# An order planner that lets VectorE and GpSimd exclude each other, four operands moved to PSUM, and one more projection pair ahead of a pointwise product

## The chip, the core and the metric

The kernel runs on one core of a Trainium2 chip. The metric is device time in microseconds (us) of one execution; lower is better. The core has five engines with queues of their own: PE (TensorE, matmuls and transposes), DVE (VectorE), ACT (ScalarE), POOL (GpSimd) and SP (SyncE, which here only issues DMAs). An engine works through its own queue strictly in the order in which the program was written, so one late operand holds back everything behind it.

## What is computed

One layer over 2048 tokens of width 1024, with 16 learned meta tokens put in front:

```
u = rms_norm(h, pre_g)
glu_a, glu_b, conv_gate, q, k, v, sb_gate = split(u @ w_in)      # 7 x 512 columns
c = glu_a * sigmoid(glu_b)
c = silu(layer_norm(causal_depthwise_conv(c, 31 taps)))
c = (c @ w_pw2 + b_pw2) * silu(conv_gate)
s = stick_breaking_attention(q, k, v) * silu(sb_gate)            # 8 heads x 64
out = h + rms_norm(concat[c, s] @ w_out, post_g)
```

All of it is float32. Each product is made from three matmuls of high and low parts (hi x hi, hi x lo, lo x hi), so every operand is split: ACT copies it to a rounded type (`uh`, `hi`, `ah`), and DVE or POOL subtracts that from the original (`ul`, `lo`, `al`).

## The kernel before

**Tiles and stages.** The tokens are worked in four chunks of 512 columns (`TC`), channels on the 128 partitions. For each chunk: `in_proj` forms the glu pairs (`pairs`: the sigmoid half `G_B`, then the linear half `G_A`, for four groups `j` of 128 channels), then k, v and q; `attention` is the main stream of the chunk; beside it run, as filling work, `sb_gate`, the output projection of the chunk before, `conv_norm`, and `tail`, which holds `conv_gate`, a number of glu pairs of the next chunk (`BEFORE[c + 1]`, line 75), `conv_out` (the product with `w_pw2`, "pw2" for short) and the rest of the next `in_proj`. One projection group is 8 x 3 matmuls of 512 columns.

**The turn.** The normalised input of a chunk lies in two tiles `uh` and `ul`, of which there is one each. While the last `conv_gate` group of a chunk uses part k of them, `renew` asks for part k of the next chunk: `part_in` lets ACT write `uh` and DVE write `ul` by a SCALAR_TENSOR_TENSOR whose two wide operands, `t` and `uh`, lie in SBUF. The next pair needs these parts at once.

**The rates.** The row of rms rates of a chunk is made on PE by transposing a column broadcast along the free axis (`spread` for chunk 0, `spread_later` for the others), copied by ACT from PSUM into the SBUF tile `row`, and multiplied by DVE into the eight 128x512 parts of the input: `times` for chunk 0 (tiles `pr`, eight), `scale` for the others (tiles `tok`, eight a chunk). Chunk 0 starts before its rates are known: its first three pairs run on unscaled parts, and `once_more` forms the parts again from the scaled ones.

**Who does what.** DVE does the convolution as 31 taps for most groups (`conv`, run in the PSUM bank `cv`), the scans of the attention (`pr`) and most low parts; POOL does the low parts of the weights (`w<-wr,w`, but for the seven slabs named in `FIRST`, which DVE does), the taps of some groups (`conv_apart`), and a few sums. `swish` in `conv_norm` lets ACT write a sigmoid into an SBUF tile `ev`, and DVE combines it with the normalised value. In `meta_keys` the contribution of the meta tokens comes from PE in a PSUM tile `pj`; DVE adds it to the attention output `sr` and multiplies by the gate `gt`, both in SBUF.

**PSUM.** Eight banks of 128x512: two named `mm` (projections), four named `T`, taken in turn (attention scores, transposes, and what else needs a bank for a moment), one `av` (attention output of a head) and one `cv` (running convolution).

**What sets the order.** The program is written out by a planner that keeps an account of every engine's time. `Engine.issue` charges each instruction with a cost (`pe_cost`, `dve_cost`, `act_cost`, `pool_cost`), begins it when its engine is free in the account and its operands are ready in the account, and notes when its result will be there. `merge` takes the next piece of the main, the filling or the extra stream, whichever is ready by the account, keeping the two first to a pace given in `SHARES`; `step` runs pending small operations when they are ready and adds convolution taps while the account has DVE less than 1.5 us (`LAGS`) ahead of PE. So a wrong cost does not change a result: it changes the order in which the engines' queues are written, and where PE then finds an operand late. Nearly all instructions are written by line 211 (`issue`), which is why the profile's rows are told apart by their tiles.

Of the kernel before, what the change touches and what calls it, by code (L numbers as in the profile page):

```python
# [19 lines left out]
P = 128  # L20
# [3 lines left out]
NM = 16  # L24
# [47 lines left out]

BEFORE = 0, 1, 0, 0

SHARES = (
    [(29.8, 169.2)], [(73.1, 214.4)], [(116.0, 214.4)], [(125.1, 97.4), (160.4, 126.3)],
# [8 lines left out]
class Clock:  # L87
# [3 lines left out]
    def __init__(self):  # L91
        self.ready, self.used, self.free, self.rings, self.bufs = {}, {}, {}, {}, {}
        self.dma = 0.0
        self.soon = []

        self.here = ()
# [71 lines left out]
class Engine:  # L168
# [7 lines left out]
    def __getattr__(self, name):  # L176
        call = getattr(self.engine, name)

        def issue(out, *args, **kw):
            c = self.clock  # L180
            outs = [out] + [kw[k] for k in ("accum_out",) if k in kw]
            ins = [a for a in (*args, *kw.values()) if hasattr(a, "ap")]

            for a in (*ins, *outs):
                for e in c.writers(a, c.here):
                    self.run(e)
            for a in outs:
                for e in c.readers(a, c.here):
                    self.run(e)
            near = [a for a in ins if a.space != DRAM]  # L190
            when = max([c.at(a) for a in near] + [c.free.get(out.name, 0.0)]) + self.wait
            if self.gap:
                self.gap(when)
            n = max(int(np.prod(a.shape[1:])) for a in (out, *args) if hasattr(a, "shape"))
            busy, late = self.cost(name, n, kw)
            start = max(self.now, when)
            self.now = start + busy
            self.work += busy
            done = self.now + late
            if name == "dma_start":  # L200
                size = 4 * int(np.prod(out.shape))
                c.dma = max(c.dma, start + 1.6) + size / 370e3
                done = c.dma + 0.7
                if start > 30.0:
                    done += 2.5 if out.name.startswith("wr") else 1.0
            for a in outs:
                c.ready.setdefault(a.name, {})[extent(a)] = done
            for a in (*outs, *near):
                late = 3.0 if a.name.startswith("wr") and start > 30.0 else 0.0
                c.used[a.name] = max(c.used.get(a.name, 0.0), done + late)  # L210
            return call(out, *args, **kw)  # L211

        return issue


def pe_cost(name, n, kw):
    return max(4.5e-3 + n * 4.41e-4, 0.108 if n >= 64 else 0.06), 0.19


def dve_cost(name, n, kw):  # L220
# [39 lines left out]
def trunk(ctx: ExitStack, tc: tile.TileContext, x, xturn, xlater, meta, cpack, post_g, wpack, out):  # L260
# [272 lines left out]
                there.add(key)  # L533
            order.append((key, n, kept, save))
    todo_w = deque(order)
    FIRST = [len(order) - i - 1 for i in (0, 2, 3, 4, 5, 6, 7)]
    whole = [key for key, n, kept, save in order if not kept]
    at = {key: i for i, key in enumerate(slab_keys())}
    todo_raw = deque(whole)
# [100 lines left out]
    def load_first_in():  # L640

        uh, ul = u_now
        load_raw(1)
        sp.dma_start(cp, cpack)
        mt = T("pr", [P, KD, NM], PR)
        sp.dma_start(mt, xturn[:, :, :NM])
        keep["turned", 0] = 0
        ts = []  # L650
        for k in range(KD):
            ts.append(T("pr", [P, TC], PR))
            sp.dma_start(ts[k], xturn[:, k, NM:])
            when(lambda k=k: part_in(0, k, ts[k], uh, ul), [ts[k], cp])
            if k == 0:
                load_raw(2)

        def meta_in():
            hi, lo = uh[:, :, 0:NM], ul[:, :, 0:NM]
            act.activation(hi, mt, AF.Copy)  # L660
            dve.tensor_tensor(lo, mt, hi.bitcast(F32), op=ALU.subtract)

        def meta_times():
            dve.tensor_tensor(
                mt, mt, preg.unsqueeze(2).to_broadcast([P, KD, NM]), op=ALU.mult
            )
            meta_in()
            keep["meta"] = True

        when(meta_times, [mt, cp])  # L670
        load_raw()
        measured = []

        def fetch(i):
            t = tok()
            for b in range(2):
                tb = 2 * i + b
                sp.dma_start(t[:, b], x[tb * P : (tb + 1) * P, :])
                when(lambda b=b, tb=tb: measure(t[:, b], tb), [t[:, b]], tag="ev")

        def fetch_meta():
            m = T("q2", [P, D], 2)[:NM]
            sp.dma_start(m, meta)
            when(lambda: measure(m, NTB), [m], tag="ev")

        fetch(0)
        fetch_meta()
        when(lambda: fetch(1), [], date=7.5)

        def measure(t, tb):  # L690
            n = t.shape[0]
            junk = T("ev", [P, D], EV, BF16)
            act.activation(
                junk[:n], t, AF.Square, scale=D ** -0.5, accum_out=squares[:n, tb : tb + 1]
            )
            measured.append(tb)
            if len(measured) == NTB + 1:
                when(rates, [squares], [rate0])

        def rates():  # L700
            pool.tensor_scalar(squares, squares, 1e-6, None, op0=ALU.add)
            pool.tensor_tensor(
                rate0, squares, nhalf.to_broadcast([P, NTB + 1]), op=ALU.pow
            )
            when(spread, [rate0], [row])

        def spread():
            pt = PT("cv", [P, TC])
            for tb in range(NTB):
                pe.transpose(  # L710
                    pt[:, tb * P : (tb + 1) * P], rate0[:, tb : tb + 1].to_broadcast([P, P]),
                    ident,
                )
            pm = PT("av", [P, TC])[:, :NM]
            pe.transpose(
                pm, rate0[:NM, NTB : NTB + 1].to_broadcast([NM, P]), ident[:NM, :NM]
            )
            act.activation(row[:, NM:], pt, AF.Copy)
            act.activation(row[:, :NM], pm, AF.Copy)
            keep["row"] = True  # L720
            for go in waiting:
                go()
            for k in range(KD):
                when(
                    lambda k=k: times(k), [ts[k], row], [ts[k]], dve, pe.now + 3.0 + 1.5 * k
                )
            dve.tensor_tensor(
                mt, mt, row[:, :NM].unsqueeze(1).to_broadcast([P, KD, NM]), op=ALU.mult
            )

        scaled = []

        def times(k):
            dve.tensor_tensor(ts[k], ts[k], row[:, NM:], op=ALU.mult)
            scaled.append(k)

        def once_more(k):

            if k == 0:
                keep["turned", 0] = 0  # L740
                when(meta_in, [mt], date=pe.now)
            when(lambda: part_in(0, k, ts[k], uh, ul), [ts[k]], date=pe.now)

        keep["scaled"] = lambda: "row" in keep and len(scaled) == KD
        keep["once more"] = once_more
# [33 lines left out]

    def to_spread(c):  # L780
        if ("half", c) in keep and ("rates", c) in keep:
            when(lambda: spread_later(c), [later], [row], tag="T")

    def times_rate(c, k):
        t = xs[c, k]
        when(lambda: scale(c, k, t), [t, row], [t])

    def scale(c, k, t):
        dve.tensor_tensor(t, t, row[:, NM:], op=ALU.mult)
        keep["scaled", c, k] = True  # L790
        renewed(c)

    def spread_later(c):
        pt = PT("T", [P, TC])
        for tb in range(NTB):
            n = (c - 1) * NTB + tb
            pe.transpose(
                pt[:, tb * P : (tb + 1) * P], later[:, n : n + 1].to_broadcast([P, P]), ident
            )
        act.activation(row[:, NM:], pt, AF.Copy)  # L800
        keep["row", c] = True
        for k in range(KD):
            if (c, k) in xs:
                times_rate(c, k)
# [307 lines left out]
    def conv_norm(c, accs):  # L1112
# [56 lines left out]
                )  # L1169
        yield need(given=lambda: len(done) == 2 * NJ)  # L1170
        def swish(j):
            b, y, sg = lnb[:, j : j + 1], accs[j], ev()[:, :TC]
            act.activation(sg, y, AF.Sigmoid, bias=b)
            when(
                lambda: dve.scalar_tensor_tensor(y, y, b, sg, op0=ALU.add, op1=ALU.mult),
                [y, sg], [y],
            )

        for j in range(NJ):
            when(  # L1180
                lambda j=j: swish(j), [accs[j]], [accs[j]], date=pe.now + 1.5 * j, tag="ev"
            )
        keep["normed", c] = True

# [293 lines left out]
    def meta_keys(c, h0, h1, mixs):  # L1478
# [66 lines left out]
        for j in js:  # L1545
# [6 lines left out]
            pe.matmul(pj, vm[:, 0, j, :], al, start=False, stop=False)  # L1552
            pe.matmul(pj, vm[:, 1, j, :], ah, start=False, stop=True)
            hold.difference_update((sr.name, gt.name))
            dve.tensor_tensor(sr, pj, sr, op=ALU.add)
            dve.tensor_tensor(sr, sr, gt, op=ALU.mult)
            hi = T("mixs", [P, TC], 8, F32R)
            lo = T("mixs", [P, TC], 8, F32R)
            split(sr, hi, lo)
# [409 lines left out]
```

## Time and profile before

| | |
|---|---|
| median of 3 runs | 1333.38 us (1331.79 to 1334.39) |
| the profiled execution | 1335.07 us |
| its span, first to last instruction | 1333.2 us |
| instructions | 21888 |
| PE, PE weight load, DVE, ACT, POOL busy | 97%, 84%, 77%, 55%, 50% of the span |
| mean granted TensorE clock | 0.993 of full |
| DMA | 300.76 MB, mean 226 GB/s |

The span leaves out 1.9 us around the first and last instruction. "Busy" of PE counts matmuls whose ends are modelled, so a wait shorter than a matmul's modelled tail does not show as idle time. A row of instruction groups reads: line, engine, operation, tiles out <- in, shape, count | busy us in all, mean ns of one | idle time of the engine just before them and what ended it. A row of the timeline reads: start, duration, engine, operation, tiles, count, and in brackets the idle time before it with what ended it. A row of waits reads: us in total, times, longest us. In rows of windows every engine has its busy time with its count of instructions, then come the granted clock, the share of time the DMA engines moved data, and GB/s.

### The profile page before, as it was taken

The page shows a single profiled execution, that of the slowest core. Times are in us where ns is not written, and L with a number is a line of the kernel's source. Part 1 is how long each engine was busy: PE and PEld are TensorE (multiplying, and loading weights), DVE is VectorE, ACT ScalarE, POOL GpSimd, SP SyncE. Part 2 cuts the span into 40 slices and gives each one's busy share as a digit, 9 for nine tenths or more (in the row PEclk, how much of TensorE's full clock was granted, in tenths as well). Part 3 has the DMA queues.
Part 4 walks back from the last instruction along what each step waited for, and adds up shares of the span by engine and source line. Part 5 has one row for each costly group of instructions (what it writes and reads, how often), then busy time and mean ns, then how long its engine had stood idle before and what let it go on. Part 6 is the DMA issues. An engine that isn't in the chain of part 4 may idle for free.

```text
span 1333.2 us, 21888 instructions
## 1 busy us (share of the span) xinstructions
PE 1299.6 (97%) x7498; PEld 1115.9 (84%) x7498; DVE 1025.9 (77%) x1438; ACT 735.0 (55%) x1470; POOL 667.3 (50%) x780
## 2 busy tenths in 40 slices
PE   8899998999999999999999999999999999999995
PEld 8898886888789987888889988888877899988895
DVE  4999987998993488984586478885549889798864
ACT  6444454444455443567745444578776566655542
POOL 3545466777667631688831242399787121231400
PEclk9999998999999999999999999999999999999998
DMA  6676885899978995676755697666666556686644
GB/s 227 197 248 214 252 266 197 305 312 323 319 239 261 289 344 180 192 240 221 248 190 176 174 337 222 180 184 217 196 197 210 156 149 181 196 277 199 207 147 155
DMA packets 167470, 300.76 MB, mean 226 GB/s; under 512 B 17840, under 2 KB 72304, under 8 KB 167360
## 3 DMA queue, kind: packets, MB, share of 16 engines
q1 hardware_dynamic: 154208, 253.49, 61.4%
q0 software_dynamic: 13152, 45.88, 9.0%
q8 instruction: 59, 0.97, 0.3%
q14 instruction: 51, 0.42, 0.1%
HBM read 221.85 MB, written 77.46 MB: 225 GB/s over the span
## 4 chain that ended last, share of the span: by engine, by line
PE 84%; DVE 8%; DMA 3%; ACT 2%; issue 1%; POOL 1%; DVEq 0%; SPq 0%; POOLq 0%; ACTq 0%
PE mm L211 54%; PE T L211 20%; PE av L211 9%; DVE ul L211 2%; DVE tok L211 2%; DVE pr L211 1%; DVE cv L211 1%; DMA ev<-x 1%; DMA w<-wscr 1%; ACT ev L211 1%; DMA out<-tok 0%; DMA tok<-xlater 0%; PE cv L211 0%; DMA wr<-wscr 0%; DVE al L211 0%
## 5 line engine op out<-in xcount | busy, mean ns | idle before, releaser
L211 PE MATMUL mm<-uh,w 128*128 128x512 f32 (+1 forms) x1936 | 622.3, 378 | 4.5 <-DVE ehl L211 2.8
L211 PEld LDWEIGHTS mm<-uh,w 128*128 128x128 f32 x1936 | 354.7, 190 | 65.5 <-DVE ehl L211 2.8
L211 PE MATMUL mm<-ul,w 128*128 128x512 f32 (+1 forms) x968 | 362.7, 375 | 5.3 <-DVE ul L211 5.3
L211 DVE TENSOR_TENSOR al<-T,ah 128x512 fp32r<-128x512 f32 (+3 forms) x323 | 194.5, 602 | 142.3 <-ACT ah L211 140.9
L211 DVE TENSOR_TENSOR_SCAN pr<-T,pr,zcol 128x512 f32<-128x512 f32 x192 | 245.1, 1277 | 45.9 <-ACT T L211 43.5
L211 ACT ACTIVATE ah<-T 128x512 fp32r<-128x512 f32 (+3 forms) x323 | 171.7, 532 | 170.6 <-PE T L211 169.5
L211 DVE SCALAR_TENSOR_TENSOR cv<-ct,cp,cv 128x512 f32<-128x512 f32 x319 | 239.2, 750 | 7.0
L211 ACT ACTIVATE T<-T 128x512 f32<-128x512 f32 (+2 forms) x320 | 167.5, 525 | 95.2 <-PE T L211 91.5
L211 POOL TENSOR_TENSOR w<-wr,w 128x512 fp32r<-128x512 f32 x133 | 174.9, 1319 | 89.3 <-ACT w L211 88.1
L211 POOL TENSOR_TENSOR acc<-acc,pd 128x512 f32<-128x512 f32 x150 | 195.3, 1302 | 42.7 <-ACT pd L211 36.3
L211 PEld LDWEIGHTS mm<-ul,w 128*128 128x128 f32 x968 | 184.2, 190 | 34.5 <-DVE ul L211 8.6
L211 PE MATMUL T<-kk,q 128*128 128x512 f32 (+2 forms) x640 | 194.8, 387 | 1.5 <-DVE pr L211 1.4
L211 PE MATMUL T<-ident,pr 128*128 128x128 f32 x1088 | 171.2, 272 | 0.3 <-DVE al L211 0.2
L211 PEld LDWEIGHTS T<-ident,pr 128*128 128x128 f32 x1088 | 134.1, 140 | 31.3 <-DVE al L211 1.0
L211 DVE TENSOR_TENSOR_SCAN pr<-T,tri 128x128 f32<-128x128 f32 (+3 forms) x128 | 103.8, 814 | 19.5 <-ACT T L211 18.4
L211 PEld LDWEIGHTS T<-kk,q 128*128 128x128 f32 x640 | 105.3, 189 | 15.2 <-DVE pr L211 1.6
L211 PE MATMUL av<-ah,vk 128*128 128x512 f32 (+1 forms) x320 | 117.2, 366 | 0.0
L211 PE MATMUL av<-al,vk 128*128 128x512 f32 (+1 forms) x320 | 117.1, 366 | 0.0
L211 ACT ACTIVATE pd<-ct,cp 128x512 f32<-128x512 f32 x150 | 106.3, 717 | 16.5 <-POOL acc L211 15.7
L211 ACT ACTIVATE w<-wr 128x512 fp32r<-128x512 f32 x140 | 86.9, 626 | 48.2 <-PE mm L211 21.0
L211 POOL COPY cm<-pr 128x1 f32<-128x1 f32 x120 | 26.6, 222 | 148.0 <-DVE pr L211 147.6
L211 POOL TENSOR_TENSOR ev<-ev 64x512 f32<-64x512 f32 (+2 forms) x46 | 55.9, 1216 | 68.1 <-ACT ev L211 52.2
(191 smaller groups left out, 1589.9 us busy)
## 6 DMA issues: line engine op xcount, KB each, us to landing
w<-wscr SPq DMA_DIRECT2D x150, 512.0 KB, 4.0
wr<-wpack SPq DMA_DIRECT2D x140, 256.0 KB, 4.5
wscr<-w POOLq DMA_DIRECT2D x68, 512.0 KB, 5.0
kk<-kscr SPq DMA_DIRECT2D x80, 256.0 KB, 4.8
vk<-vscr SPq DMA_DIRECT2D x80, 256.0 KB, 3.9
q<-qscr SPq DMA_DIRECT2D x64, 256.0 KB, 5.6
vscr<-mixs SPq DMA_DIRECT2D x32, 256.0 KB, 3.3
qscr<-ehl SPq DMA_DIRECT2D x32, 256.0 KB, 3.3
```

Source lines behind the costliest of these rows:

```text
L211: return call(out, *args, **kw)
```

## The change

Five edits:

1. In the planner's account, a DVE or POOL instruction with at least two wide input operands (64 elements or more) in SBUF may not overlap one of the other engine; it is begun when the other's ends.
2. `pe_cost` charges a matmul of n columns with n x 0.4537 ns in place of 4.5 ns + n x 0.441 ns (512 columns: 232.3 ns, before 230.3 ns).
3. The rates stay in PSUM for chunk 0 (`times`) and chunk 1 (`scale`): the bank is now `av`, ACT's copy into `row` falls away for chunk 1 and stays for chunk 0, where other work reads it. The sigmoid of `swish` is written into a `T` bank. In `meta_keys` the sum is formed in place in `pj`, and the gate's product reads it there.
4. `BEFORE[1]` is 2 in place of 1: two glu pairs of chunk 1 stand ahead of pw2 of chunk 0.
5. `FIRST` holds the second weight slab too: DVE forms its low part, and the raw slab that follows is asked for at once instead of 2 us later.

```diff
-BEFORE = 0, 1, 0, 0
+BEFORE = 0, 2, 0, 0
...
+            wide = [a for a in near if a.space != PSUM and int(np.prod(a.shape[1:])) >= 64]
+            if self.cost in (dve_cost, pool_cost) and len(wide) > 1:
+                for a, b in c.shared.get(dve_cost if self.cost is pool_cost else pool_cost, ()):
+                    if a < start + busy and b > start:
+                        start = b
+                c.shared.setdefault(self.cost, deque(maxlen=16)).append((start, start + busy))
             self.now = start + busy
...
-    return max(4.5e-3 + n * 4.41e-4, 0.108 if n >= 64 else 0.06), 0.19
+    return max(n * 4.537e-4, 0.108 if n >= 64 else 0.06), 0.19
...
-    FIRST = [len(order) - i - 1 for i in (0, 2, 3, 4, 5, 6, 7)]
+    FIRST = [len(order) - i - 1 for i in range(8)]
...
-            pt = PT("cv", [P, TC])
+            pt = PT("av", [P, TC])
...
-            pm = PT("av", [P, TC])[:, :NM]
+            pm = PT("cv", [P, TC])[:, :NM]
...
-                    lambda k=k: times(k), [ts[k], row], [ts[k]], dve, pe.now + 3.0 + 1.5 * k
+                    lambda k=k: times(k, pt), [ts[k], pt], [ts[k]], dve, pe.now + 3.0 + 1.5 * k
...
-            dve.tensor_tensor(ts[k], ts[k], row[:, NM:], op=ALU.mult)
+            dve.tensor_tensor(ts[k], ts[k], rates, op=ALU.mult)
...
-            when(lambda: spread_later(c), [later], [row], tag="T")
+            when(lambda: spread_later(c), [later], [row], tag="av" if c == 1 else "T")
...
-        dve.tensor_tensor(t, t, row[:, NM:], op=ALU.mult)
+        dve.tensor_tensor(t, t, rates, op=ALU.mult)
...
-        act.activation(row[:, NM:], pt, AF.Copy)
-        keep["row", c] = True
+        keep["row", c] = pt
+        if c > 1:
+            act.activation(row[:, NM:], pt, AF.Copy)
+            keep["row", c] = row[:, NM:]
...
-            b, y, sg = lnb[:, j : j + 1], accs[j], ev()[:, :TC]
+            b, y, sg = lnb[:, j : j + 1], accs[j], PT("T", [P, TC])
...
-            dve.tensor_tensor(sr, pj, sr, op=ALU.add)
-            dve.tensor_tensor(sr, sr, gt, op=ALU.mult)
+            dve.tensor_tensor(pj, pj, sr, op=ALU.add)
+            dve.tensor_tensor(sr, pj, gt, op=ALU.mult)
```

More of the change, by code (lines that the diff above doesn't have):

```diff
@@ L93, in __init__ @@
         self.dma = 0.0
+        self.shared = {}
         self.soon = []
@@ L731, in load_first_in, with times @@
         scaled = []
-        def times(k):
-            dve.tensor_tensor(ts[k], ts[k], row[:, NM:], op=ALU.mult)
+        def times(k, rates):
+            dve.tensor_tensor(ts[k], ts[k], rates, op=ALU.mult)
             scaled.append(k)
@@ L781, in to_spread, with scale @@
         if ("half", c) in keep and ("rates", c) in keep:
-            when(lambda: spread_later(c), [later], [row], tag="T")
+            when(lambda: spread_later(c), [later], [row], tag="av" if c == 1 else "T")
     def times_rate(c, k):
         t = xs[c, k]
-        when(lambda: scale(c, k, t), [t, row], [t])
-    def scale(c, k, t):
-        dve.tensor_tensor(t, t, row[:, NM:], op=ALU.mult)
+        rates = keep["row", c]
+        when(lambda: scale(c, k, t, rates), [t, rates], [t])
+    def scale(c, k, t, rates):
+        dve.tensor_tensor(t, t, rates, op=ALU.mult)
         keep["scaled", c, k] = True
@@ L793, in spread_later @@
     def spread_later(c):
-        pt = PT("T", [P, TC])
+        pt = PT("av" if c == 1 else "T", [P, TC])
         for tb in range(NTB):
@@ L1180, in conv_norm @@
             when(
-                lambda j=j: swish(j), [accs[j]], [accs[j]], date=pe.now + 1.5 * j, tag="ev"
+                lambda j=j: swish(j), [accs[j]], [accs[j]], date=pe.now + 1.5 * j, tag="T"
             )
```

## The prediction

> **What bounds the kernel now.** I read the page's head first, then PE's waits, then windows around them.
>
> ```profile
> span 1333.2 us, 21888 instructions
> PE 1299.6 (97%) x7498; PEld 1115.9 (84%) x7498; DVE 1025.9 (77%) x1438; ACT 735.0 (55%) x1470; POOL 667.3 (50%) x780
> PEclk9999998999999999999999999999999999999998
> ```
>
> PE is busy 1299.6 of 1333.2 us. No edit removes a matmul, so the most that the change can win is PE's waiting, and slow-clock time. The third row shows the clock below full in slice 7 and in the last. The waits of PE over the whole span:
>
> ```profile
> PE mm L211 <- DVE ul L211: 5.3, 6, 2.4
> PE mm L211 <- DVE ehl L211: 2.8, 4, 1.6
> PE T L211 <- DVE ul L211: 2.6, 4, 0.8
> PE mm L211 <- DMA w<-wscr: 1.4, 1, 1.4
> PE T L211 <- DVE pr L211: 1.4, 1, 1.4
> PE T L211 <- POOL ev L211: 1.4, 3, 0.6
> ```
>
> Almost everything that PE waited for came from DVE: `ul`, the low part of the input, and `ehl`, the sigmoid half of a glu pair or the split of k. Asked for 30 to 85 us, the waits view gives the second and third row unchanged, so these 2.8 + 2.6 = 5.4 us lie in the front. For 193 to 216 us, chunk 0's turn to chunk 1, it gives this, followed by windows:
>
> ```profile
> PE mm L211 <- DVE ul L211: 4.3, 4, 2.4
> ```
>
> ```profile
> 30.00:58.00 28.00, 24.52 (x189) 23.08 (x188) 27.80 (x38) 13.78 (x27) 16.45 (x13) 1.00 0.57 186
> 58.00:85.00 27.00, 25.06 (x202) 24.48 (x202) 26.49 (x37) 12.39 (x26) 11.37 (x10) 1.00 0.66 211
> 193.00:209.00 16.00, 11.81 (x53) 8.45 (x51) 12.93 (x12) 12.56 (x25) 13.74 (x13) 0.99 0.71 222
> 209.00:216.00 7.00, 6.81 (x17) 5.38 (x18) 3.12 (x7) 2.02 (x4) 4.02 (x6) 0.54 0.31 119
> ```
>
> In the front DVE is busy 54.3 of 55 us: it is the bound there. At the turn PE loses 4.3 us to waits, and right behind them the clock is at 0.54 for 7 us, which costs 7 x 0.46 = 3.2 us more. Front and turn together are 5.4 + 7.5 = 12.9 us; the other waits are 1.4 + 1.4 + 1.4 and smaller ones, about 5. The rest of the span is PE at work, the first operands on their way, and the closing stage, which is not touched.
>
> **Why DVE is late.** The groups of DVE in 30 to 85 us, and single rows of the timeline:
>
> ```profile
> L211 DVE TENSOR_TENSOR pr<-pr,row 128x512 f32<-128x512 f32 x8 | 8.8, 1110 | 0.0
> L211 DVE TENSOR_TENSOR tok<-tok,row 128x512 f32<-128x512 f32 x8 | 8.5, 1106 | 0.0
> ```
>
> ```profile
> 33.15 5.93 POOL L211 TENSOR_TENSOR w<-wr,w 128x512 fp32r<-128x512 f32 x4
> 36.35 1.58 DVE L211 TENSOR_TENSOR pr<-pr,row 128x512 f32<-128x512 f32 x1
> 40.99 0.68 DVE L211 TENSOR_TENSOR pr<-pr,row 128x512 f32<-128x512 f32 x1
> ```
>
> The same product takes 1.58 us while POOL works on two SBUF operands, and 0.68 when POOL is idle. That is exclusion: the second to come waits. The account charges 0.06 + 512 x 1.055e-3 = 0.60 us in both cases. The other kind of operand, over the whole run:
>
> ```profile
> L211 DVE TENSOR_TENSOR acc<-acc,T 128x512 f32<-128x512 f32 x16 | 9.9, 679 | 0.0
> L211 DVE TENSOR_TENSOR tok<-T,tok 128x512 f32<-128x512 f32 x12 | 8.1, 674 | 0.0
> L211 DVE TENSOR_TENSOR tok<-tok 128x512 f32<-128x512 f32 x12 | 11.2, 931 | 0.4
> L211 DVE SCALAR_TENSOR_TENSOR acc<-acc,cp,ev 128x512 f32<-128x512 f32 x16 | 11.9, 766 | 0.0
> L211 DVE SCALAR_TENSOR_TENSOR acc<-acc,cp,T 128x512 f32<-128x512 f32 x16 | 11.0, 741 | 0.0
> ```
>
> With one operand in PSUM a product takes 679 or 674 ns on average over the run, what the uncontended one took; with both in SBUF it is 931.
>
> **The change, part by part.**
>
> *Rates in PSUM.* Chunk 0: 8 x (1.110 - 0.679) = 3.4 us less DVE time, chunk 1: 8 x (1.106 - 0.679) = 3.4 us, both ahead of 85 us. ACT's copy for chunk 1 falls away, off the path. Of the 5.4 us that PE waits here, the 2.6 for `ul` stand behind the first eight products and the 2.8 for `ehl` mostly behind the second eight, so 6.8 us of relief stands against 5.4. What is late next: the `once_more` parts still have both wide operands in SBUF, and DVE has taps to fill every gap. I take 4.5 us won; bounds 0 (taps take the freed time) and 5.4.
>
> [...]
>
> *Swish and meta sums.* 16 x (766 - 741) ns = 0.4 us and 12 x (931 - 674) ns = 3.1 us of DVE, spread over four turns where PE mostly has other work: 0 on the path. The price is room. The sigmoid now holds one of four `T` banks until DVE has used it:
>
> ```profile
> 196.61 0.72 ACT L211 ACTIVATE ev<-acc,cp 128x512 f32<-128x512 f32 x1
> 209.26 0.73 DVE L211 SCALAR_TENSOR_TENSOR acc<-acc,cp,ev 128x512 f32<-128x512 f32 x1
> 389.72 0.71 ACT L211 ACTIVATE ev<-acc,cp 128x512 f32<-128x512 f32 x1
> 393.34 1.19 DVE L211 SCALAR_TENSOR_TENSOR acc<-acc,cp,ev 128x512 f32<-128x512 f32 x1
> L211 PE MATMUL T<-kk,q 128*128 128x512 f32 (+2 forms) x640 | 194.8, 387 | 1.5 <-DVE pr L211 1.4
> ```
>
> The last of chunk 0 would have held it from 196.61 to 209.99, 13.4 us; the second of chunk 1 from 389.72 to 394.53, 4.8 us. The last row's 640 matmuls are two to a bank: 320 score banks, and about as many for transposes, in the span of 1333 us, one per 2.1 us. Banks are taken in turn, so a bank held longer than three others take (6.3 us) stops the attention. The account sees it and takes other work or runs the product earlier. I take 1.0 us lost; bounds 0 and, for all sixteen, the rival below.
>
> *The account at the turn.*
>
> ```profile
> L211 DVE SCALAR_TENSOR_TENSOR ul<-tok,cp,uh 128x512 fp32r<-128x512 f32 x8 | 11.3, 1452 | 3.2 <-ACT uh L211 3.2
> 204.57 4.57 DVE L211 SCALAR_TENSOR_TENSOR ul<-tok,cp,uh 128x512 fp32r<-128x512 f32 x2
> 206.08 1.29 POOL L211 TENSOR_TENSOR mixs<-acc,mixs 128x512 fp32r<-128x512 f32 x1
> 207.32 1.26 POOL L211 TENSOR_TENSOR w<-wr,w 128x512 fp32r<-128x512 f32 x1
> 209.19 0.80 PE L211 MATMUL mm<-ul,w 128*128 128x512 f32 x1 [2.43 <-DVE ul L211]
> 209.79 1.05 PE L211 MATMUL mm<-uh,w 128*128 128x512 f32 x2
> 215.84 0.63 PE L211 MATMUL mm<-uh,w 128*128 128x512 f32 x2
> ```
>
> The first row groups 193 to 210 us: eight parts at 1452 ns, where the account charges 0.125 + 0.540 = 0.665 and the same operation with one SBUF operand takes 741. The last two parts took 4.57 us, because two POOL operations ran back to back before DVE got in; PE waited 2.43 us for them and then ran at half speed (two matmuls in 1.05 us, later 0.63). With the exclusion the account puts these parts later, so `merge` should write attention pieces there instead of a projection that will stand. The parts stay as slow as they are; only what PE does meanwhile changes, and chunk 0's attention also needs DVE. Of 4.3 + 3.2 = 7.5 us I take about half, 4.0; bounds 0 (nothing else is ready) and 7.5.
>
> [...]
>
> *Two pairs ahead of pw2.* Two groups of 24 matmuls change places with pw2: PE's sum stays. Weight slabs change places with them; a late slab cost 1.4 us once in this trace (`w<-wscr`), so bounds are 1.4 lost or won; I take 0, hidden by the slabs loaded ahead. Convolution input of group 1 is there some 11 us earlier (48 matmuls at the 0.232 us that the diff charges), which helps DVE's supply of taps only.
>
> *Slab 1 on DVE.*
>
> ```profile
> 8.83 1.26 DVE L211 SCALAR_TENSOR_TENSOR ul<-pr,cp,uh 128x512 fp32r<-128x512 f32 x1 [0.43 <-ACT uh L211]
> 8.17 1.37 POOL L211 TENSOR_TENSOR w<-wr,w 128x512 fp32r<-128x512 f32 x1 [3.71 <-ACT w L211]
> ```
>
> It adds 0.68 us to DVE at 8 us and takes away the POOL operation that made `ul` 1.26 in place of 0.74: between 0 and 0.2 lost, I take 0. The raw slab asked for earlier is one DMA issue on SP, ahead of nothing that PE waits for first.
>
> *Cost of a matmul and the new order.* 2 ns in 232 moves no wait by itself, but the whole plan is written anew: the some 5 us of scattered waits behind 216 us may vanish or double, and I take 0.
>
> **Sum.** 4.5 + 4.0 - 1.0 = 7.5 us. On the profiled execution, 1335.07 - 7.5 = 1327.6 (span 1325.7); that execution lies 1.7 above the median, so from the median of 1333.38 it is **1325.9**.
>
> **Rivals.** (a) *All of front and turn goes*, T banks cost nothing: 5.4 + 7.5 = 12.9, giving 1320.5. For it: the relief in the front exceeds the waits. Against: the turn's `ul` parts stay contended. 17%.
>
> (b) *Given back.* DVE's freed time is filled by taps, the turn keeps its waits because attention needs DVE too, or POOL again gets in twice where the account foresees once: 1.5 to 2 us are left, 1331.5. For it: DVE busy 54.3 of 55 us, and an account that charges single exclusions where the last two parts paid more. 15%.
>
> (c) *Slower: the T banks become the bound.* What attention ran on PE between the late parts, in the groups of 193 to 210 us:
>
> ```profile
> L211 PE MATMUL T<-kk,q 128*128 128x256 f32 x4 | 0.9, 304 | 0.0
> L211 PE MATMUL T<-ident,pr 128*128 128x128 f32 x5 | 0.9, 271 | 0.0
> ```
>
> If sigmoids hold two of four banks there, these 1.8 us have to go elsewhere, and one more stretch of half clock costs 3.2. In the other chunks twelve sigmoids hold a bank for 4.8 us: 12 x 4.8 / 4 banks = 14.4 us if banks are the bound throughout, half of it, 7.2, where fill is at hand. With the front won in full: 1333.4 + 12.2 - 5.4 = 1340.2. It decides from where three more banks are asked for within one hold, 6.3 us at the mean pace: of the two holds shown, one passes that. 16%.
>
> (d) The forecast, 1325.9, from 1321 to 1330.7: 52%.
>
> **How the numbers follow.** About 0.2% (2.7 us) is what a measurement can tell from no change. Faster is (a) and (d), 69%; same is (b), 15%; slower is (c), 16%. The range reaches from (a) with most of the scattered waits gone as well, 1317, to 1337, short of (c) at its full price; some 15% is left out.
>
> **What would show it.** In the changed trace: `pr<-pr` and the first eight `tok` products at about 0.68 us; no wait of PE on `ehl` over 0.5 us before 85 us; DVE less than 54 of 55 us busy there, or PE's first attention matmul 4 to 5 us earlier. At the turn: attention matmuls between the first parts, waits on `ul` under 2.5 us, and no stretch of clock near 0.5. Wrong it would be if PE shows new waits on `T` tiles behind the sigmoids, if the clock still falls there, or if waits behind 216 us grow beyond 5 us.

## The result and the profile after

The changed kernel takes 1321.89 us (median of 4 runs, 1320.56 to 1323.13), the kernel before 1333.89 (4 runs, 1331.79 to 1334.91): a ratio of 0.9912 with an interval of 0.9895 to 0.9929, 12.0 us less. The profiled execution took 1323.13 us, the slowest of the four. The page of the changed kernel, where `issue` now stands in line 218:

```profile
span 1321.4 us, 21882 instructions
PE 1294.5 (98%) x7498; PEld 1114.0 (84%) x7498; DVE 1013.1 (77%) x1439; ACT 735.3 (56%) x1469; POOL 659.0 (50%) x779
PEclk9999999999999999999999999999999999999998
```

PE has the same 7498 matmuls and the dip of the clock in slice 7 is gone. What PE still waited for, over the whole span (two rows of the start, 1.8 us each, and three of 0.6 us or less are left out):

```profile
PE T L218 <- DVE pr L218: 3.2, 4, 1.6
...
PE T L218 <- DVE ul L218: 1.6, 2, 0.9
PE T L218 <- POOL ev L218: 1.1, 2, 0.6
PE mm L218 <- DVE ul L218: 1.0, 2, 0.7
PE mm L218 <- DMA w<-wscr: 0.7, 1, 0.7
```

No wait on `ehl` is left. Windows of the front, the turn, and the seven us that had run at 0.54 of the clock (columns as in the part before):

```profile
30.00:58.00 28.00, 26.41 (x214) 25.95 (x213) 27.45 (x43) 16.34 (x31) 15.81 (x14) 1.00 0.61 201
58.00:85.00 27.00, 27.00 (x223) 26.83 (x222) 25.21 (x41) 12.24 (x25) 12.82 (x12) 1.00 0.74 241
196.00:212.00 16.00, 15.17 (x73) 12.24 (x73) 11.93 (x18) 9.38 (x20) 14.42 (x18) 1.00 0.59 195
209.00:216.00 7.00, 7.00 (x35) 5.71 (x34) 6.82 (x11) 3.51 (x7) 5.10 (x8) 1.00 1.01 283
```

Between 30 and 85 us the waits view of the changed kernel has the one row of 1.6 us on `ul`, 5.4 before: 3.8 us less. At the turn (180 to 216 us) it has 0.7 us, 4.3 before: 3.6 less, and the 3.2 us of slow clock, the prediction's estimate, are gone too. That is 10.6 of the 11.8 us by which the spans differ. Behind 216 us the waits sum to 6.1 us, 5.4 before, so nothing was won there. What is left, 1.2 us of the spans and the 0.7 us lost there, some 2 us, these views do not place.

In the front, the DVE groups between 26 and 85 us show what the edit to the rates did:

```profile
L218 DVE TENSOR_TENSOR pr<-pr,av 128x512 f32<-128x512 f32 x8 | 5.4, 680 | 0.0
L218 DVE TENSOR_TENSOR tok<-tok,av 128x512 f32<-128x512 f32 x8 | 5.0, 682 | 0.5 <-DMA tok<-xlater 0.5
```

Sixteen products at 680 and 682 ns, where they had taken 1110 and 1106: 6.8 us of DVE, as forecast. At the turn, the DVE group of 186 to 200 us, then rows of the timeline at its end:

```profile
L218 DVE SCALAR_TENSOR_TENSOR ul<-tok,cp,uh 128x512 fp32r<-128x512 f32 x8 | 7.1, 923 | 0.1
```

```profile
195.73 1.61 POOL L218 TENSOR_TENSOR w<-wr,w 128x512 fp32r<-128x512 f32 x1 [2.68 <-ACT w L218]
196.11 1.77 DVE L218 SCALAR_TENSOR_TENSOR ul<-tok,cp,uh 128x512 fp32r<-128x512 f32 x1
197.81 0.73 DVE L218 SCALAR_TENSOR_TENSOR acc<-acc,cp,T 128x512 f32<-128x512 f32 x1
197.86 1.32 POOL L218 TENSOR_TENSOR mixs<-acc,mixs 128x512 fp32r<-128x512 f32 x1
```

The low parts became faster, 923 ns in place of 1452. The last one meets one POOL operation instead of a line of them: POOL's splits of the normalised values (`mixs<-acc,mixs`) now start behind it. The swish's product (`acc<-acc,cp,T`) runs beside the first of them, reads PSUM and takes 0.73 us, so it is not stopped.

### The profile page after: what moved, and what is told of

Its sections match the earlier page's. It is cut to its first block, busy times and chain, and to the rows that moved or that the text cites. A ratio compares the mean times of both kernels' runs of the same rounds, so it can differ in the third digit from the quotient of the medians.

```text
span 1321.4 us, 21882 instructions
## 1 busy us (share of the span) xinstructions
PE 1294.5 (98%) x7498; PEld 1114.0 (84%) x7498; DVE 1013.1 (77%) x1439; ACT 735.3 (56%) x1469; POOL 659.0 (50%) x779
## 4 chain that ended last, share of the span: by engine, by line
PE 86%; DVE 5%; DMA 4%; ACT 1%; POOL 1%; issue 1%; SPq 0%; DVEq 0%; ACTq 0%; POOLq 0%
PE mm L218 56%; PE T L218 21%; PE av L218 9%; DVE ul L218 2%; DMA ev<-x 2%; DVE tok L218 1%; DVE pr L218 1%; POOL acc L218 1%; DMA tok<-xlater 1%; DMA w<-wscr 0%; ACT ev L218 0%; DMA out<-tok 0%; DVE cv L218 0%; PE cv L218 0%; DMA tok<-gscr 0%
## 5 line engine op out<-in xcount | busy, mean ns | idle before, releaser
L218 POOL TENSOR_TENSOR w<-wr,w 128x512 fp32r<-128x512 f32 x132 | 171.3, 1302 | 92.7 <-ACT w L218 90.1
```

## The experiments

Each kernel is the kernel before or the changed one with the edit shown; medians and ratios are against runs of the kernel before on the same chip.

**The changed kernel without the exclusion.**

```diff
-            wide = [a for a in near if a.space != PSUM and int(np.prod(a.shape[1:])) >= 64]
...
-                c.shared.setdefault(self.cost, deque(maxlen=16)).append((start, start + busy))
```

> The changed kernel without the exclusion in the account; all its other edits stay. Theory 1 (operands in PSUM win the front, the account wins the turn): waits of PE on ehl and ul between 30 and 85 us stay at 1 to 2.5 us, as in the changed kernel, and the turn near 190 to 216 us shows waits on ul of 3 us or more, with or without a stretch of half clock; time 1326 to 1331, 4 to 9 us over the changed kernel's 1321.9. Rival (the turn was won by anything that writes the plan anew, the second pair or the swish in PSUM): the turn stays clean and the time is within 2 us of the changed kernel.

1326.8 us, ratio 0.9958 (0.9947 to 0.9970). The front keeps its gain, one row of 1.6 us. The turn is that of the kernel before, by its waits and its DVE group of 183 to 207 us:

```profile
PE mm L212 <- DVE ul L212: 4.3, 4, 2.0
```

```profile
L212 DVE SCALAR_TENSOR_TENSOR ul<-tok,cp,uh 128x512 fp32r<-128x512 f32 x8 | 11.2, 1452 | 3.0 <-ACT uh L212 3.0
```

So without the account's edit the turn is not won, although swish, sums and the second pair are all there. Theory 1 holds as far as this goes. The clock did not fall at this turn: it was full (1.00) from 195 to 207 us.

**The kernel before with the rates alone.**

```diff
-            pt = PT("cv", [P, TC])
+            pt = PT("av", [P, TC])
...
-            dve.tensor_tensor(ts[k], ts[k], row[:, NM:], op=ALU.mult)
+            dve.tensor_tensor(ts[k], ts[k], rates, op=ALU.mult)
```

> The kernel before with the rates of chunks 0 and 1 read from PSUM, the banks exchanged as in the change, and no other edit. Theory 1: the eight products of chunk 0 and of chunk 1 take about 0.68 us each, waits between 30 and 85 us fall from 5.4 to 1 to 2.5 us, the turn keeps waits of 3 us or more: 1327 to 1331. Rival (freed DVE time is filled with taps): waits in the front stay above 4 us, time 1332 to 1335.

1326.68 us, ratio 0.9961 (0.9947 to 0.9976), the waits of 30 to 85 us and of 180 to 216 us:

```profile
PE T L211 <- DVE ul L211: 1.6, 2, 0.9
```

```profile
PE mm L211 <- DVE ul L211: 4.4, 4, 2.4
```

Rates alone take away the same 3.8 us of waits in the front as the whole change and leave the turn. The freed time was not eaten by taps. The time fell by 6.3 us, so some 2.5 us more than these waits, which were not placed. This kernel and the one above are equal within their intervals, so without the account the other edits add nothing that can be measured.

**The kernel before with the exclusion alone.**

```diff
+            wide = [a for a in near if a.space != PSUM and int(np.prod(a.shape[1:])) >= 64]
+            if self.cost in (dve_cost, pool_cost) and len(wide) > 1:
...
```

> The kernel before with the exclusion in the account and no other edit. Theory 1: the front keeps most of its waits (4 to 6 us by the waits between 30 and 85 us, since the products with the rates still have both operands in SBUF, although the account now expects that), the turn's waits on ul fall under 2.5 us and the half clock is gone: 1325 to 1330. Rival: the turn keeps 3 us or more of waits on ul, time 1331 to 1335. A second rival (the account alone is enough, since it also keeps taps out of the front): the front's waits fall to 2 us as well, and the time is 1322 to 1325.

1336.3 us, ratio 1.0022 (1.0012 to 1.0031): slower, and outside what any of the three theories expected. The front's waits fell to 1.8 us by the account alone, with the rates still in SBUF: chunk 1's products take 908 ns there in place of 1106 and the `once_more` parts 947 in place of 1090, and two taps fewer stand among them. The waits on `ul` at the turn are gone too, with the swish still in SBUF, but another hole opened. The end of chunk 0's last convolution in the kernel before, in this one, and this one's window behind the first pair:

```profile
173.76 0.75 DVE L211 SCALAR_TENSOR_TENSOR acc<-ct,cp,cv 128x512 f32<-128x512 f32 x1
```

```profile
197.57 0.74 DVE L218 SCALAR_TENSOR_TENSOR acc<-ct,cp,cv 128x512 f32<-128x512 f32 x1
...
205.00:225.00 20.00, 11.11 (x69) 8.54 (x67) 19.07 (x30) 16.22 (x36) 9.73 (x17) 0.99 0.75 216
```

The account now has DVE later, so it admits taps later: 24 us at the last tap of chunk 0. The norm and the swish wait for it, pw2 waits for them, the single pair is used up, and PE idles 8.9 of 20 us. No rival of the prediction had this.

**The same with two pairs ahead of pw2.**

```diff
-BEFORE = 0, 1, 0, 0
+BEFORE = 0, 2, 0, 0
```

> The kernel before with the exclusion in the account and two pairs ahead of the product with w_pw2. The kernel with the exclusion alone was slower, and its trace shows PE without fill from 205 to 225 us, since the last convolution of chunk 0 ended at 198 us and the norm came late. Theory 1 (the account pushes taps back, and a second pair covers that): PE idle in the stretch of 20 us behind the first pair falls from 9 us to under 4 and the time is 1324 to 1330. Rival (the hole is DVE's backlog, which a pair does not shorten, it only moves): the hole comes back behind the second pair, time 1333 to 1337.

1330.24 us, ratio 0.9976 (0.9965 to 0.9988): 6 us better than the exclusion alone. Its trace shows PE busy without a gap from 205 to 218 us, and then this window and this wait, of 180 to 250 us:

```profile
218.00:226.00 8.00, 2.94 (x19) 2.58 (x18) 7.90 (x8) 3.87 (x8) 7.26 (x9) 0.97 0.35 132
```

```profile
PE T L218 <- DVE pr L218: 5.1, 1, 5.1
```

Both theories are half right: the pair covers a part, and 5.1 us of the hole come back behind it. Of 8.9 us idle, 5 are left, where theory 1 asked for under 4. The turn itself has no wait on `ul` here either. The low parts there, in the DVE group of 183 to 197 us:

```profile
L218 DVE SCALAR_TENSOR_TENSOR ul<-tok,cp,uh 128x512 fp32r<-128x512 f32 x8 | 8.4, 1114 | 0.0
```

The swish products, in SBUF in this kernel, come at 213 to 225 us, long behind these parts, so they and the splits that follow them do not meet them.

**Rates and exclusion together, nothing else.**

```diff
+            if self.cost in (dve_cost, pool_cost) and len(wide) > 1:
...
-            pt = PT("cv", [P, TC])
+            pt = PT("av", [P, TC])
```

> The kernel before with the rates in PSUM and the exclusion in the account, nothing else. Theory 1 (the freed 6.8 us of DVE pay for the taps that the account pushes back): last convolution of chunk 0 ends before 175 us, the turn is clean, time 1323 to 1328. Rival (the account costs the same 3.4 us here as alone): 1329 to 1332.

1345.05 us, ratio 1.0087 (1.0074 to 1.0100), the slowest of all, where 1323 to 1328 was expected. The taps are in time here (the last convolution ends at 170 us), but at the turn the waits of 180 to 250 us and the last two low parts read:

```profile
PE mm L218 <- DVE ul L218: 4.1, 2, 3.3
```

```profile
195.23 6.05 DVE L218 SCALAR_TENSOR_TENSOR ul<-tok,cp,uh 128x512 fp32r<-128x512 f32 x2
```

Behind 250 us PE waits 16.4 us, where it was 5.4 in the kernel before: on `pr` (3.7), on weights (`ACT w` 2.0, `POOL w` 1.8) and others. The trace has three stretches of slow clock between the start and the closing stage (196 to 208, 320 to 328 and 512 to 520 us), one of them at the turn; its mean over the span is 0.988, where the changed kernel's is 0.996. Why the new plan has these holes behind 250 us was not followed up. So two edits of which one wins 6 us and one loses 3 lose 12 together: the parts cannot be added.

**The changed kernel with swish and meta sums back in SBUF, and with the swish alone back.**

```diff
-            b, y, sg = lnb[:, j : j + 1], accs[j], PT("T", [P, TC])
+            b, y, sg = lnb[:, j : j + 1], accs[j], ev()[:, :TC]
...
-                lambda j=j: swish(j), [accs[j]], [accs[j]], date=pe.now + 1.5 * j, tag="T"
+                lambda j=j: swish(j), [accs[j]], [accs[j]], date=pe.now + 1.5 * j, tag="ev"
...
-            dve.tensor_tensor(pj, pj, sr, op=ALU.add)
-            dve.tensor_tensor(sr, pj, gt, op=ALU.mult)
+            dve.tensor_tensor(sr, pj, sr, op=ALU.add)
+            dve.tensor_tensor(sr, sr, gt, op=ALU.mult)
```

> The changed kernel with the sigmoid of the swish and the meta sums back in SBUF. Theory 1 (as forecast: 3.5 us of VectorE off the path against a T bank held longer): within 2 us of the changed kernel's 1321.9, waits on T tiles from VectorE 1 us less. Rival (the T banks cost more): 1317 to 1319.5. Second rival (contention at the turn comes back): 1324 to 1328, low parts at the turn above 1.2 us.

> The changed kernel with the sigmoid of the swish back in SBUF, the meta sums in PSUM as in the change. With both back, the last two low parts at the turn took 5.91 us behind four GpSimd operations in a row, PE waited 3.3 us for them and chunk 1 had holes of 4.4 and 2.6 us. Theory 1 (the sigmoid in PSUM is what clears the turn, since VectorE no longer stands in GpSimd's line there): most of the 19 us comes back with the swish alone, time 1335 to 1342, low parts at the turn above 1.2 us. Rival (the meta sums did it, or each half): 1322 to 1331.

Both back: 1341.18 us, ratio 1.0057 (1.0045 to 1.0069), outside all three expectations. The swish alone back (first two pairs of lines): 1339.94, ratio 1.0054 (1.0042 to 1.0067), where theory 1 expected it. So the swish is nearly all of it: beside the exclusion and the rates, 18 us hang on where sixteen sigmoids lie. The edit does two things at once: the product no longer meets GpSimd, and the account no longer charges it as an operation that may have to wait. Which of the two carries how much of the 18 us was not told apart. The timeline of the kernel with only the swish back, at the turn and in chunk 1, shows where PE stands:

```profile
196.21 4.32 DVE L218 SCALAR_TENSOR_TENSOR ul<-tok,cp,uh 128x512 fp32r<-128x512 f32 x1
196.26 2.50 POOL L218 TENSOR_TENSOR mixs<-acc,mixs 128x512 fp32r<-128x512 f32 x2
198.72 1.25 POOL L218 TENSOR_TENSOR w<-wr,w 128x512 fp32r<-128x512 f32 x1
200.58 0.79 PE L218 MATMUL mm<-ul,w 128*128 128x512 f32 x1 [3.28 <-DVE ul L218]
...
304.44 10.24 DVE L218 SCALAR_TENSOR_TENSOR cv<-ct,cp,cv 128x512 f32<-128x512 f32 x13
314.93 0.33 PE L218 MATMUL av<-al,vk 128*128 128x128 f32 x1 [4.35 <-DVE al L218]
```

At the turn two swish products had run just ahead of the last low parts. Their two splits on POOL and the low part of a weight came in a row, and one low part of the input waited through all three: 4.32 us, PE 3.28, then half clock (0.50 from 200 to 204 us, two matmuls in 1.05 us and later in 0.62). In chunk 1 thirteen taps stand ahead of one low part of the attention, and PE waits 4.35 us for it, 2.57 a little later. Why the account saw room for thirteen taps there was not followed up.

**The changed kernel with one pair ahead of pw2.**

```diff
-BEFORE = 0, 2, 0, 0
+BEFORE = 0, 1, 0, 0
```

> The changed kernel with one pair ahead of the product with w_pw2, as before, in place of two. Theory 1: the second pair does nothing for the turn, which lies ahead of it; time within 2 us of the changed kernel's 1321.9. Rival (the second pair gives the low parts or the swish the time that they lacked): waits at the turn come back, 1325 to 1330.

1326.02 us, ratio 0.9949 (0.9937 to 0.9961): 4 us of the change hang on the second pair, but not at the turn, where the wait is the changed kernel's 0.7 us. Waits of 250 to 360 us in this kernel, and in the changed one:

```profile
PE T L218 <- DMA kk<-kscr: 1.6, 1, 1.6
PE av L218 <- DVE al L218: 1.2, 1, 1.2
PE T L218 <- DVE ehl L218: 0.9, 1, 0.9
```

```profile
PE T L218 <- DVE pr L218: 1.6, 1, 1.6
```

Neither theory had chunk 1, where PE waits 2.1 us more: theory 1 has the turn right and the time wrong, the rival the time right and the place wrong. The other 2 us are not placed: over the whole span the waits of PE are as long in this profile as in the changed kernel's (12.4 and 12.3 us), and the two profiled spans differ by only 1.6 us.

**A flat charge in place of the exclusion.**

```diff
-            if self.cost in (dve_cost, pool_cost) and len(wide) > 1:
...
+            if self.cost is dve_cost and len(wide) > 1:
+                busy += 0.4
```

> The changed kernel with the exclusion replaced by a flat 0.4 us on every VectorE instruction with two wide SBUF operands, no matter what GpSimd does. Theory 1 (the account wins by knowing where the two meet): the eight low parts at the turn stay at 1.2 us or more on average and PE waits 2 us or more for them; time 1324 to 1329. Rival (any slower VectorE in the account keeps PE from running into the parts): the same as the changed kernel within 2 us, 1320 to 1324.

1331.14 us, ratio 0.9984 (0.9975 to 0.9992). The low parts at the turn (groups of 186 to 210 us) and PE's wait of 180 to 216 us:

```profile
L215 DVE SCALAR_TENSOR_TENSOR ul<-tok,cp,uh 128x512 fp32r<-128x512 f32 x8 | 11.7, 1508 | 3.0 <-ACT uh L215 3.0
```

```profile
PE mm L215 <- DVE ul L215: 3.3, 3, 2.0
```

A VectorE that is slower by this much in the account does not do it, and is 4 us worse than no charge at all. What helps at the turn is knowing when the two engines meet; other flat charges were not tried. The time lies beyond both expectations; 3.1 us of the surplus is a wait in the start, where the rates come late on POOL.

**The old cost of a matmul, and slab 1 on GpSimd again.**

```diff
-    return max(n * 4.537e-4, 0.108 if n >= 64 else 0.06), 0.19
+    return max(4.5e-3 + n * 4.41e-4, 0.108 if n >= 64 else 0.06), 0.19
...
-    FIRST = [len(order) - i - 1 for i in range(8)]
+    FIRST = [len(order) - i - 1 for i in (0, 2, 3, 4, 5, 6, 7)]
```

> The changed kernel with the old cost of a matmul in the account and slab 1's low part on GpSimd again. Theory 1 (both are side matters): within 2 us of the changed kernel's 1321.9. Rival (2 ns on 230 is enough to move the plan into another set of holes, as the other undone parts did): 1326 or more.

1323.61 us, ratio 0.9930 (0.9917 to 0.9942), which overlaps the changed kernel's. Side matters, as expected; the two were undone together, so this gives their sum.

**Two placebos: 10 ns in the account, in either kernel.**

```diff
-    return (0.06 if name == "tensor_tensor" else 0.125) + 1.055e-3 * n, 0.085
+    return (0.06 if name == "tensor_tensor" else 0.125) + 1.055e-3 * n, 0.095
```

> A placebo: the changed kernel with 10 ns more on the time after which the account has a VectorE result ready (0.095 in place of 0.085 us); no operation changes. Theory 1 (the edits win what they win): within 2 us of the changed kernel's 1321.9. Rival (any plan written anew lands several us away, so that a good part of the 12 us is the luck of one plan): 1325 to 1340.

> The same placebo on the kernel before. Theory 1: within 2 us of the kernel before's 1333.4. Rival: 1327 or less, or 1337 or more, with the turn's waits or the holes behind it changed.

The changed kernel: 1320.87 us, ratio 0.9910 (0.9897 to 0.9924). The kernel before: 1333.11, ratio 1.0005 (0.9996 to 1.0014). Both plans were written anew and stay within some 1 us of their own. Their waits at the turn (180 to 216 us), changed kernel first:

```profile
PE mm L218 <- DVE ul L218: 0.7, 1, 0.7
```

```profile
PE mm L211 <- DVE ul L211: 5.0, 2, 4.2
```

So the 12 us are hardly the luck of one plan: this one small disturbance keeps the holes of the one and the clean turn of the other.

## Why the prediction was right

The way and the range were right; 1325.9 was forecast, 1321.9 measured. By its own steps:

- *What bounds.* Right. Everything that can be placed was won where PE waited for DVE in the front and at the turn; matmuls stayed as they were. (The prediction's list of waits leaves out two rows of the start, 1.8 and 1.7 us; they are 1.8 and 1.8 in the changed kernel.)
- *Rates in PSUM.* Right: 680 ns as forecast, 3.8 us of waits gone where 4.5 was taken, and the run with the rates alone shows the whole of it. The exclusion alone took 3.6 us of the same waits away, so in the full change the front is won twice over; the changed kernel without the rates was not run.
- *The account at the turn.* The term was mis-sized: 4.0 taken, against 3.6 us of waits and the estimated 3.2 of slow clock, 6.8 in all, near the upper bound of 7.5. Not all of that is the exclusion's: undoing it alone costs 4.9 us, and the clock stayed full (1.00) at that kernel's turn. The sentence that the parts "stay as slow as they are" was wrong. The order that the account wrote kept POOL out of DVE's way, and the parts themselves fell from 1452 to 923 ns. Without the exclusion the turn keeps waits of 4.3 us. With it, and with the rates early, the swish has to be in PSUM as well: with the swish in SBUF one wait of 3.3 us is left. With the exclusion but without the rates no wait on `ul` is left at the turn with the swish in SBUF either, because the swish then comes long behind it.
- *Swish and meta sums.* The step that failed in sign: "0 on the path", and 1.0 lost for room. In the changed kernel the swish in PSUM carries 18 us, and the meta sums 1 at most, within the intervals. These 18 us belong to the exclusion's plan: without the exclusion, swish, sums, pair and the rest add nothing to the rates that can be measured. The price in room did not appear: at the turn a bank was held for 6.4 us at most, from ACT's sigmoid to the end of the product, where `ev` had been held for 13.4, and PE has no wait on a `T` tile within 100 us behind any of the four groups of sigmoids.
- *Two pairs.* 0 taken; 4 us hang on it, of which 2.1 are waits in chunk 1, and beside the exclusion alone it wins 6.
- *The scattered waits* behind 216 us: 0 taken, 0.7 us more measured. At 6.1 us they stand beyond the 5 us that the prediction named as a sign of being wrong. That sign was badly set, since the kernel before has 5.4.

That the sum came near is in part luck: turn and pairs were taken too small, and the swish, without which this plan does not win, was taken as a loss. A sum over parts is the wrong form here. Done one at a time on the kernel before, the parts give -6.3 (rates), +3.4 (exclusion) and, for these two together, +11.7. The rival that would have been needed is the one that the exclusion alone showed: a more cautious account pushes the taps back, and the filling work runs out. In the full change that hole is closed: the last convolution of chunk 0 ends at 172 us, and the second pair stands behind the turn. Rival (c), the T banks, did not happen.

One meeting with a POOL operation made a low part of the changed kernel take 1.77 us, where one that met none took 0.74. The engine kept waiting is not always next in line: with the swish in SBUF a low part took 4.32 us through three operations of the other.

## What to carry to other kernels

A planner that knows which operations of two engines hold each other up in the trace (here 1.77 us for a low part that met one, 0.74 alone) can win where they meet, but its caution moves other work, and that has to be paid for with work that can fill. Here it lost 3 us alone, and a second pair made that a gain of 3. Beside the rates it lost 12, and it won there only once the sigmoid of the swish was moved to PSUM. So test it in the combination that is to be used. Move one operand of a VectorE operation to PSUM first where GpSimd is busy and PE waits for VectorE; here the sixteen products with the rates then took 678 and 680 ns in place of 1110 and 1106, and that alone gave half of the gain, 6.3 us. And before crediting single edits of a planned order, write the plan anew with a placebo: here one placebo moved each kernel by some 1 us or less, the side matters came to 2, and the other edits but the meta sums, done or undone one at a time, to 3 to 18.

## What the runs showed of the hardware

A waiting VectorE operation often did not get its turn between GpSimd operations that follow each other at once: one took 4.32 us through three with the swish in SBUF, one 3.46 us through two in the kernel before. It is no fixed rule. In the front of the kernel before, four GpSimd splits of weights follow each other at 33.15, 34.40, 36.10 and 37.34 us and take 1.28, 1.74, 1.28 and 1.74 us. Two VectorE products with the rates that begin during the first and the third take 1.44 and 1.58 us and end 0.56 and 0.55 us behind them, so each went ahead of the split that followed. What decides was not found.

A short copy of VectorE from SBUF to SBUF, which no edit touches, took longer as well: 355 ns on average in the changed kernel, 189 in the kernel before. The groups before and after, and one such copy of the changed kernel with the two GpSimd operations beside it (the second ends at 857.45 us, the copy at 857.48):

```profile
L211 DVE COPY ct<-ct 128x30 f32<-128x30 f32 x12 | 2.3, 189 | 0.0
```

```profile
L218 DVE COPY ct<-ct 128x30 f32<-128x30 f32 x12 | 4.3, 355 | 0.0
854.75 2.70 POOL L218 TENSOR_TENSOR acc<-acc,pd 128x512 f32<-128x512 f32 x2
856.55 0.93 DVE L218 COPY ct<-ct 128x30 f32<-128x30 f32 x1
```

It has one input only, so the account does not charge it.

And the length of the longest wait did not decide whether the granted clock fell. It fell at the turn of the kernel before, after four waits of 4.3 us in all, the longest 2.4 (0.54 from 209 to 216 us). It stayed full (1.00 from 195 to 207 us) in the kernel without the exclusion, through four waits of 4.3 us in all, the longest 2.0. With the flat charge it fell right behind the first wait of the turn, of 2.0 us (0.70 from 196 to 200 us).
